# Attention and mLSTM block on one core: V, O and Z projections with time on the partitions, branch outputs turned by DMA

## Chip, cores and metric

The kernel runs on one core of a Trainium2 chip. The metric is the device time of one execution in microseconds; the median of several runs is given, and a profiled execution supplies the trace.

## What is computed

One layer of a hybrid block on x (1024 time steps, 1024 channels), batch 1, everything in float32 at the interface:

```
xn = rmsnorm(x)
(da_q, da_k, da_v, da_z, ml_q, ml_k, ml_v, ml_o, ml_z, ml_i, ml_f, gate_a, gate_m) = split(xn @ w_in)
y_a = diff_attention(da_q, da_k, da_v) * silu(da_z)          # 8 heads, two softmaxes per head,
                                                             # rmsnorm over the head's 128 channels
y_m = mlstm(conv_silu(ml_q), conv_silu(ml_k), ml_v, ml_i, ml_f)   # 8 heads, chunked, layer norm per head
y_m = sigmoid(ml_o) * y_m * silu(ml_z)
merged = sigmoid(gate_a) * (y_a @ w_pa) + sigmoid(gate_m) * (y_m @ w_pm)
out = rmsnorm(x + merged @ w_out)
```

Each head has 128 value channels, and 1024 steps are eight blocks of 128. Every large product is done in float16 with both operands split into a high and a low half: high x high, high x low and low x high are accumulated, three matmuls where one would do in one precision.

## The kernel before

**Layout.** X, the normed input, lies in SBUF turned: channels on the partitions, time along the row, as f16 high and low halves. A *unit* (class `Unit`) is 256 output columns of a projection: two blocks of 128. `plain_unit` (lines 334 to 346) computes it with the weights stationary and X moving: for each half of the time (`th`, 512 steps) and each block (`cb`), 8 channel blocks x 3 matmuls of 512 columns are accumulated in one of three PSUM banks (`pp`), so a unit is 96 matmuls, and its result has output channels on the partitions and time along the row. `post` of the unit's consumer then empties the bank on ScalarE and VectorE.

**Units and consumers.** `c_avz` takes attention's V and Z of one head. V is split into f16 halves (lines 559 and 560) in `vT` and turned to rows (time on the partitions) by one transposing DMA (line 634). Z is gated in place by tanh (lines 545 and 546). `c_mvo` takes the mLSTM's V and O: V is copied to `vT` (line 345) and turned by eight TensorE transposes (`to_rows`, line 554) and a scaled ScalarE copy (line 555); O multiplies into the z gate (lines 696 and 697). `c_mz` does Z of two mLSTM heads. `c_aqk` and `c_mqk` do the Q and K projections.

**Side work.** Beside the projection of the next head runs a generator of the current one: `attention(h, plan)` or `mlstm(h)`. Lists such as `PLAN_A` give the slot (about three matmuls of projection) at which each piece is traced. In attention the piece `v` multiplies probabilities by V (lines 867 to 869) into a single PSUM bank (`pvp`) holding four blocks of time; `f` computes factors on GpSimd (lines 874 to 876); `o` scales the bank into `on` (line 880), with time on the partitions; `t` turns it by four TensorE transposes (line 885), and `finish_y` multiplies by the gate (line 528) and splits into the f16 halves of `Y` (lines 529 and 530). In the mLSTM the normed rows `num` (line 987) are turned by four TensorE transposes (line 992) into the same `finish_y`.

**Order.** Y is first read by the units `pa` and `pm`, which multiply by `w_pa` and `w_pm`; the former follow the last attention head, the latter the last mLSTM head. The final projection `wo` has the merged result stationary (128x128) and 256 columns of weights moving. Weights of a unit are loaded into three buffers (line 226, by SyncE's queue), squared and summed for a scale (ScalarE, line 245), and split (lines 257 and 259) while the unit before is computed. Work is traced in program order and then placed on each engine's in-order queue by the framework's planner, which goes by modelled times, so that the order on an engine can differ from the program's. SyncE's queue holds nearly all DMA issues: weight loads, the Q and K copies, attention's transposing DMAs (line 859).

Of the kernel before, what the change touches and what calls it, by code (L numbers as in the profile page):

```python
# [9 lines left out]
F16 = mybir.dt.float16  # L10
# [7 lines left out]
P = 128  # L18
# [30 lines left out]
def block_kernel(ctx, tc, x, norm_w, w_in, lam, subln_w, rel_bias, conv_w, conv_b, b_if,  # L49
# [38 lines left out]
    def p_ps():  # L88
        return pp.tile([P, 512], F32, tag="pp", name=nm("pp"))
# [4 lines left out]
    def m_ps():  # L94
        return pmi.tile([P, 512], F32, tag="pmi", name=nm("pmi"))
# [7 lines left out]
    def b3(ap):  # L103
        return ap.rearrange("p (a b) -> p a b", b=P)
# [168 lines left out]
    def wplain(w, i, c):  # L273
        hi, lo = w.parts[i // 2]
        return hi[:, i % 2, c], lo[:, i % 2, c]
# [16 lines left out]
        return t[:, 0, i % 2, :], t[:, 1, i % 2, :]  # L292

    def y_src(base):
        return lambda i, th: (Y[base + i][:, 0, th, :], Y[base + i][:, 1, th, :])

    class Unit:
        def __init__(self, kind, idx, srcs, rowscale=None, src=x_src, keep=False):
            self.kind, self.idx, self.srcs = kind, idx, srcs
            self.rowscale, self.src, self.keep = rowscale, src, keep  # L300
            self.w = self.prepping = None

        def start_load(self):
# [30 lines left out]
    def plain_unit(w, dst, post, src):  # L334
        for th in range(2):
            for cb in range(2):
                c = slice(cb * P, (cb + 1) * P)
                ps = p_ps()
                yield from mm3(ps, KC, lambda i: wplain(w, i, c),
                               lambda i: src(i, th), True, True)  # L340
                d = dst(cb, th) if dst else None
                if d is None:
                    d = ps
                else:
                    s.activation(d, ps, AF.Copy)  # L345
                post(cb, th, d)

    HS = [slice(0, 512), slice(512, 1024)]

    def wcols(o, n=P):  # L350
        return (w_in[0, :, o:o + n], n)
# [168 lines left out]

    isz = ctile([P, 16], p="isz")

    def finish_y(n, ps, th, gz, k):

        if n not in Y:
            Y[n] = xtile("Y")
        y32 = half_tile("y32")
        v.scalar_tensor_tensor(y32, ps, 2.0 ** k, gz[:, HS[th]], op0=ALU.mult, op1=ALU.mult)
        s.activation(Y[n][:, 0, th, :], y32, AF.Copy)
        v.tensor_tensor(Y[n][:, 1, th, :], y32, Y[n][:, 0, th, :], op=ALU.subtract)  # L530

    def sig_of(w):
        sg = sm(p="sig", bufs=8)
# [5 lines left out]
        v.tensor_scalar(hs, sg, 0.5, None, op0=ALU.mult)  # L539
        return hs  # L540

    def gate_post(tz, th, ap, hs):

        t = HS[th]
# [3 lines left out]
    def to_rows(src, dst, sg):  # L548

        def part(th):  # L550
            tp = m_ps()
            for j in range(4):
                c = th * 4 + j
                te.transpose(tp[:, j * P:(j + 1) * P], src[:, c * P:(c + 1) * P], ident)
            s.activation(dst[:, th * 4:th * 4 + 4, :P], b3(tp), AF.Copy, scale=sg)
        return [lambda: None, lambda: None, lambda: part(0), lambda: part(1)]
# [5 lines left out]
    def to_rows16(src, dst):  # L562

        def part(th):
            tp = m_ps()
            for j in range(4):
                c = th * 4 + j
                te.transpose(tp[:, j * P:(j + 1) * P], src[:, c * P:(c + 1) * P], ident)
            split16(dst, b3(tp), slice(th * 4, th * 4 + 4))
        return [lambda: None, lambda: None, lambda: part(0), lambda: part(1)]  # L570


    live = {}
# [41 lines left out]
    def c_avz(h, w):  # L615
        sg = sig_of(w)
        hs = half_of(sg)
        v.tensor_scalar(isz[:, h:h + 1], sg, 0.8 * 0.5 * 2.0 ** 17, None, op0=ALU.mult)
        tz = R(p="tz")
        vT, vr = R(F16, [P, 2, S], p="vT"), R(F16, [P, 2, NT, P], p="vr")  # L620
# [6 lines left out]
        done = [0]  # L627

        def post(cb, th, ap):
            if cb == 0:  # L630
                split16(vT, ap, HS[th])
                done[0] += 1
                if done[0] == 2:
                    nc.sync.dma_start(vr.rearrange("p a b c -> p (a b) c"), vT.rearrange("p a b -> p (a b)"),
                                      transpose=True)
            else:
                gate_post(tz, th, ap, hs)
        return None, post

    def c_mqk(h, w):  # L640
# [34 lines left out]
    def c_mvo(h, w):  # L675
        sg = sig_of(w)
        hs = half_of(sg)
        vT = R(p="vT")
# [8 lines left out]
        done = [0]  # L687

        def post(cb, th, ap):
# [8 lines left out]
        return (lambda cb, th: vT[:, HS[th]] if cb == 0 else None), post  # L698

    def c_mz(h, w):  # L700
        sg = sig_of(w)
        hs = half_of(sg)
        tz = [R(p="tz") for _ in range(2)]
# [3 lines left out]
        return None, lambda cb, th, ap: gate_post(tz[cb], th, ap, hs)  # L707
# [101 lines left out]
    def attention(h, plan):  # L809
# [67 lines left out]

        def scaled_of(qh):
            on[qh] = half_tile("on")
            v.tensor_tensor(b3(on[qh]), b3(ops[qh]), fac[qh].unsqueeze(2).to_broadcast([P, 4, P]), op=ALU.mult)  # L880

        def rows_of(qh):
            tp = m_ps()
            for j in range(4):
# [15 lines left out]
    def mlstm(h):  # L900
# [83 lines left out]
        for th in range(2):  # L984
            for c in range(th * 4, th * 4 + 4):
                with tc.high_priority(50):
                    v.tensor_scalar(num[:, c, :P], num[:, c, :P], va[:, c:c + 1], nmr[:, c:c + 1], op0=ALU.mult,
                                    op1=ALU.add)
            yield
            tp = m_ps()  # L990
            for j in range(4):
# [22 lines left out]
    def scale_m():  # L1014
# [3 lines left out]

    da_units = lambda h: [
        Unit("aqk", h, [wcols(OFF_DA[0] + h * P), wcols(OFF_DA[1] + h * P)]),  # L1020
        Unit("avz", h, [wcols(OFF_DA[2] + h * P), wcols(OFF_DA[3] + h * P)])]
    ml_units = lambda h: (
        [Unit("mqk", h, [wcols(OFF_ML[0] + h * P), wcols(OFF_ML[1] + h * P)])]
        + ([Unit("mz", h, [wcols(OFF_ML[4] + h * P, 256)])] if h % 2 == 0 else [])
        + [Unit("mvo", h, [wcols(OFF_ML[2] + h * P), wcols(OFF_ML[3] + h * P)])])
# [54 lines left out]
    for units, side, steps in phases:  # L1080
# [6 lines left out]
        for u in units:  # L1087
# [7 lines left out]
            gen = plain_unit(u.w, dst, post, u.src)  # L1095
            if n == 0:
                ifp = if_proj()
                gen = itertools.chain(gen, ifp)
# [136 lines left out]
```

## Time and profile before

| | |
|---|---|
| median of 3 runs | 1446.03 us (1445.68 to 1446.54) |
| profiled execution, its own time | 1444.22 us |
| its span, first to last instruction | 1442.4 us |
| granted TensorE clock, mean | 0.998 of full speed |
| TensorE busy | 1391.0 us, 7922 matmuls |
| VectorE, ScalarE, GpSimd busy | 844.3, 728.7, 156.5 us |
| DMA, transfers of the main queue | 32.7% of 16 engines' span |

The engines are PE (TensorE matmuls), PEld (its weight loads, which overlap), DVE (VectorE), ACT (ScalarE), POOL (GpSimd) and SP (SyncE, here only the issuing of DMAs). A row names the source line, engine, operation, output and inputs by the program's names. A busy time is the sum of a group's records; records of matmuls overlap, so the distance between starts is what one costs in a stream.

### The profile page before, as it was taken

Reading aid. Unit: us, or ns where it says so; the run is one execution under the profiler, and the core shown is the slowest. Engines: PE = TensorE matmul, PEld = TensorE weight load, DVE = VectorE, ACT = ScalarE, POOL = GpSimd, SP = SyncE. Lnnn points to the kernel's source line nnn. Section 1 sums busy time; section 2 is a strip of 40 time slices with the busy share of each in tenths; the row PEclk is TensorE's granted clock in tenths of the full one; section 3 lists DMA queues with packets and bytes.
Section 4 is the critical chain, followed back from the end, with each engine's and each line's share of the span. In section 5 each row is a group of like instructions: output and inputs, shape, how many; then the busy total and the mean of one; then the engine's idle time right before and its main releaser. Section 6 shows DMA issues by size and latency. Waiting matters only on the chain.

```text
span 1442.4 us, 21396 instructions
## 1 busy us (share of the span) xinstructions
PE 1391.0 (96%) x7922; PEld 748.4 (52%) x7922; DVE 844.3 (59%) x2214; ACT 728.7 (51%) x1469; POOL 156.5 (11%) x215
## 2 busy tenths in 40 slices
PE   5999999999999999999999999999999999999997
PEld 3445455455554545444455556455555555444686
DVE  6286967759677577333537565665665654233633
ACT  6275666556665577522444354343434344634542
POOL 2001001010010001000111111010111200122004
PEclk9999999999999999999999999999999999999999
DMA  6575557355464544434312121121212124434303
GB/s 198 71 165 127 102 109 148 83 120 112 103 141 87 112 105 141 163 128 129 95 30 88 30 88 59 54 64 44 74 30 88 59 70 145 165 95 167 119 15 118
DMA packets 215419, 145.72 MB, mean 101 GB/s; under 512 B 100145, under 2 KB 192578, under 8 KB 215314
## 3 DMA queue, kind: packets, MB, share of 16 engines
q1 hardware_dynamic: 201298, 119.08, 32.7%
q10 hardware_dynamic: 14016, 25.27, 5.2%
q8 instruction: 62, 1.02, 0.3%
q14 instruction: 43, 0.35, 0.1%
HBM read 90.12 MB, written 18.55 MB: 75 GB/s over the span
## 4 chain that ended last, share of the span: by engine, by line
PE 70%; DVE 14%; ACT 5%; DMA 4%; POOL 3%; issue 3%; SPq 0%; POOLq 0%; DVEq 0%; ACTq 0%
PE pp L329 20%; PE pp L331 20%; PE pp L330 20%; PE psb L824 3%; DVE z L834 2%; DVE wp L259 2%; DVE acc L657 2%; DMA wt<-in_w_in_dram 1%; DMA qw<-rows_d 1%; DMA z<-z 1%; PE psb L920 1%; ACT z L838 1%; ACT junk L245 1%; DVE z L849 1%; PE pvp L867 1%
## 5 line engine op out<-in xcount | busy, mean ns | idle before, releaser
L331 PE MATMUL pp<-X,wp 128*128 128x512 f16 x1408 | 533.6, 379 | 1.0 <-DVE wp L259 1.0
L329 PE MATMUL pp<-X,wp 128*128 128x512 f16 x1408 | 534.0, 379 | 0.3 <-ACT wp L257 0.3
L330 PE MATMUL pp<-X,wp 128*128 128x512 f16 x1408 | 534.0, 379 | 0.0
L331 PEld LDWEIGHTS <-wp 128*128 128x128 f16 x1664 | 162.7, 98 | 190.4 <-DVE wp L259 1.5
L329 PEld LDWEIGHTS <-wp 128*128 128x128 f16 x1664 | 162.8, 98 | 172.0 <-issue 5.3
L330 PEld LDWEIGHTS <-wp 128*128 128x128 f16 x1664 | 162.7, 98 | 162.6
L257 ACT ACTIVATE wp<-wt,sb 128x512 f16<-128x512 f32 x208 | 137.0, 711 | 112.8 <-DVE sb L138 79.6
L245 ACT ACTIVATE junk<-wt 128x1024 bf16<-128x1024 f32 x112 | 118.2, 1055 | 122.9 <-DMA wt<-in_w_in_dram 113.0
L259 DVE SCALAR_TENSOR_TENSOR wp<-wt,sb,wp 128x512 f16<-128x512 f32 x208 | 149.2, 752 | 14.7 <-ACT wp L257 13.2
L838 ACT ACTIVATE z<-z,mx 128x256 f32<-128x256 f32 (+7 forms) x128 | 98.6, 770 | 49.1 <-DVE mx L837 37.4
L834 DVE CUSTOM_DVE_ANT_0 z<-psb,BB,negc 128x256 f32<-128x256 f32 (+7 forms) x128 | 104.2, 814 | 11.2 <-PE psb L824 9.5
L331 PE MATMUL pp<-Y,wp 128*128 128x512 f16 x256 | 97.0, 379 | 0.0
L330 PE MATMUL pp<-Y,wp 128*128 128x512 f16 x256 | 97.0, 379 | 0.0
L329 PE MATMUL pp<-Y,wp 128*128 128x512 f16 x256 | 97.0, 379 | 0.0
L657 DVE SCALAR_TENSOR_TENSOR acc<-up,wcol,acc 128x512 f32<-128x512 f32 x96 | 77.0, 817 | 26.3 <-POOL acc L658 23.8
L824 PE MATMUL psb<-K,Q 128*128 128x512 f16 (+3 forms) x384 | 83.2, 325 | 5.5 <-DVE mx L834 2.9
L159 DVE TENSOR_TENSOR s<-wss 128x1 bf16<-128x1 f32 x57 | 14.2, 249 | 117.3 <-ACT junk L245 117.1
L658 POOL TENSOR_SCALAR acc<-up,wcol,cols 128x512 f32<-128x512 f32 x32 | 30.8, 966 | 394.3 <-ACT up L345 231.3
L329 PE MATMUL pp<-wo,M 128*128 128x256 f16 x256 | 69.8, 273 | 0.5 <-DVE xr L1177 0.5
L331 PE MATMUL pp<-wo,M 128*128 128x256 f16 x256 | 69.8, 273 | 0.0
L330 PE MATMUL pp<-wo,M 128*128 128x256 f16 x256 | 69.8, 273 | 0.0
L824 PEld LDWEIGHTS <-Q 128*128 128x128 f16 x384 | 37.1, 97 | 54.7 <-issue 18.1
(244 smaller groups left out, 1764.9 us busy)
## 6 DMA issues: line engine op xcount, KB each, us to landing
wt<-in_w_in_dram SPq DMA_DIRECT2D x128, 256.0 KB, 3.5
wt<-in_w_in_dram SPq DMA_DIRECT2D x24, 512.0 KB, 4.3
K<-hl SPq DMA_DIRECT2D x32, 256.0 KB, 4.1
gate_d<-tg ACTq DMA_DIRECT2D x32, 256.0 KB, 2.0
xt<-in_x_dram SPq DMA_DIRECT2D x8, 512.0 KB, 6.2
Q<-hl SPq DMA_DIRECT2D x32, 128.0 KB, 2.8
wt<-in_w_pa_dram SPq DMA_DIRECT2D x8, 512.0 KB, 5.3
ft<-gate_d ACTq DMA_DIRECT2D x16, 256.0 KB, 3.1
```

Of the source, the lines that this page charges most:

```text
L245: s.activation(j, w.wt[k], AF.Square, accum_out=ss[:, k:k + 1])
L257: s.activation(dst[0], src, AF.Copy, scale=w.sb)
L259: v.scalar_tensor_tensor(dst[1], src, w.sb, dst[0], op0=ALU.mult, op1=ALU.subtract)
L329: te.matmul(ps, wh, xh, start=(start and i == 0), stop=False, **kw)
L330: te.matmul(ps, wh, xl, start=False, stop=False, **kw)
L331: te.matmul(ps, wl, xh, start=False, stop=(stop and i == n - 1), **kw)
L657: tap = lambda j: (lambda: v.scalar_tensor_tensor(a, sh(j), wc(j), a, op0=ALU.mult, op1=ALU.add))
L658: yield lambda: g.tensor_scalar(a, sh(0), wc(0), bc, op0=ALU.mult, op1=ALU.add)
L824: te.matmul(sp[:, c:e], Q[:, p, i * P:(i + 1) * P], K[p][:, j, c:e], start=(j == 0), stop=(j == 1))
L834: v.tensor_tensor_reduce(z[:, :n], sp[:, :n], bb[:, S - n:], negc, BIG, op0=ALU.add, op1=ALU.min, accum_out=mx)
L838: s.activation(z[:, :n], z[:, :n], AF.Exp, bias=mx, scale=-1.0, accum_out=rr[:, 2 * i + p:2 * i + p + 1])
L849: v.scalar_tensor_tensor(A[:, :n], E[i, 1][:, :n], nb, A[:, :n], op0=ALU.mult, op1=ALU.add)
```

## The change

The projections whose consumers want time on the partitions are computed that way. A new `rows_unit` has X stationary (128 time steps) and 256 weight columns moving; a PSUM bank holds two time blocks x 256 columns, and `post` gets a pair of time blocks at a time. It is used for avz, mvo and mz. So V comes out as rows and the vT tiles, their transposing DMA and `to_rows` go, and the gates z and o are rows too. The branch outputs are gated while still rows (inside `scaled_of` in attention, by one multiplication in the mLSTM), split into f16 halves in a tile `y16`, and turned into Y by one transposing DMA for each half of the time. Y's layout is [half of time, high or low] in place of [high or low, half of time].

```diff
+    def rows_unit(w, post, src):
+        both = slice(0, 2 * P)
+        for n in range(NT // 2):
+            ps = p_ps()
+            for j in range(2):
+                o = slice(j * 2 * P, (j + 1) * 2 * P)
+                t = slice((n % 2 * 2 + j) * P, (n % 2 * 2 + j + 1) * P)
+                for i in range(KC):
+                    (wh, wl), (xh, xl) = wplain(w, i, both), src(i, n // 2)
+                    te.matmul(ps[:, o], xh[:, t], wh, start=i == 0, stop=False)
+                    te.matmul(ps[:, o], xh[:, t], wl, start=False, stop=False)
+                    te.matmul(ps[:, o], xl[:, t], wh, start=False, stop=i == KC - 1)
+                    if i % 2 == 1:
+                        yield
+            ps = ps.rearrange("p (j c) -> p j c", j=2)
+            for cb in range(2):
+                post(cb, slice(2 * n, 2 * n + 2), ps[:, :, cb * P:(cb + 1) * P])
...
-    def finish_y(n, ps, th, gz, k):
+    def finish_y(n, th, y32, k):
...
-        y32 = half_tile("y32")
-        v.scalar_tensor_tensor(y32, ps, 2.0 ** k, gz[:, HS[th]], op0=ALU.mult, op1=ALU.mult)
-        s.activation(Y[n][:, 0, th, :], y32, AF.Copy)
-        v.tensor_tensor(Y[n][:, 1, th, :], y32, Y[n][:, 0, th, :], op=ALU.subtract)
+        y16 = half_tile("y16").bitcast(F16)
+        s.activation(y16[:, :512], y32, AF.Copy, scale=2.0 ** k)
+        v.scalar_tensor_tensor(y16[:, 512:], y32, 2.0 ** k, y16[:, :512], op0=ALU.mult, op1=ALU.subtract)
+        nc.sync.dma_start(Y[n][:, th].rearrange("p a (c t) -> p (a c) t", t=P), y16, transpose=True)
...
     c_avz:
-                split16(vT, ap, HS[th])
-                done[0] += 1
-                if done[0] == 2:
-                    nc.sync.dma_start(vr.rearrange("p a b c -> p (a b) c"), vT.rearrange("p a b -> p (a b)"),
-                                      transpose=True)
+                split16(vr, ap, t)
             else:
-                gate_post(tz, th, ap, hs)
+                gate_post(tz, t, ap, hs)
...
     c_mvo:
-                done[0] += 1
-                if done[0] == 2:
-                    bg.extend(to_rows(vT, vr, sg))
+                s.activation(vr[:, t, :P], ap, AF.Copy, scale=sg)
             else:
-                to = main_tile("to")
+                to = main_tile("to")[:, :2 * P].rearrange("p (a b) -> p a b", b=P)
                 s.activation(to, ap, AF.Tanh, scale=hs)
-                v.scalar_tensor_tensor(gz[:, HS[th]], to, 1.0, gz[:, HS[th]], op0=ALU.add, op1=ALU.mult)
+                v.scalar_tensor_tensor(gz[:, t], to, 1.0, gz[:, t], op0=ALU.add, op1=ALU.mult)
...
     attention:
         def scaled_of(qh):
             on[qh] = half_tile("on")
-            v.tensor_tensor(b3(on[qh]), b3(ops[qh]), fac[qh].unsqueeze(2).to_broadcast([P, 4, P]), op=ALU.mult)
+            for j in range(4):
+                i = qh * 4 + j
+                v.scalar_tensor_tensor(on[qh][:, j * P:(j + 1) * P], ops[qh][:, j * P:(j + 1) * P],
+                                       fac[qh][:, j:j + 1], gz[:, i], op0=ALU.mult, op1=ALU.mult)
         def rows_of(qh):
-            tp = m_ps()
-            for j in range(4):
-                te.transpose(tp[:, j * P:(j + 1) * P], on[qh][:, j * P:(j + 1) * P], ident)
-            finish_y(h, tp, qh, gz, -17)
+            finish_y(h, qh, on[qh], -17)
...
     mlstm:
-            tp = m_ps()
-            for j in range(4):
-                te.transpose(tp[:, j * P:(j + 1) * P], num[:, th * 4 + j, :P], ident)
-            finish_y(8 + h, tp, th, gz, -18)
+            y32 = half_tile("y32")
+            v.tensor_tensor(b3(y32), num[:, th * 4:th * 4 + 4, :P], gz[:, th * 4:th * 4 + 4], op=ALU.mult)
+            finish_y(8 + h, th, y32, -18)
```

## Rows read from the trace of the kernel before

**Rows 1.** The page's first part: busy us, share of span, instruction counts by engine.
```profile
PE 1391.0 (96%) x7922; PEld 748.4 (52%) x7922; DVE 844.3 (59%) x2214; ACT 728.7 (51%) x1469; POOL 156.5 (11%) x215
```

**Rows 2.** Windows, attention then mLSTM stretch: length, engines' busy us, granted clock, DMA share, GB/s.
```profile
60.00:557.00 497.00, 479.02 (x2932) 247.57 (x2931) 357.53 (x949) 308.21 (x677) 37.42 (x62) 1.00 0.54 119
700.00:1225.00 525.00, 517.39 (x2733) 281.52 (x2732) 311.10 (x862) 223.09 (x412) 61.99 (x77) 1.00 0.22 67
```

**Rows 3.** TensorE's waits, whole span: line, releaser, total us, times, longest us.
```profile
PE pmi L554 <- ACT vT L345: 7.2, 4, 2.1
PE pvp L867 <- DVE nbeta L846: 7.2, 6, 1.4
...
PE pvp L867 <- DVE on L880: 3.1, 2, 1.6
```

**Rows 4.** Timeline of TensorE in an mvo unit: start us, length us, instruction.
```profile
740.61 0.38 PE L330 MATMUL pp<-X,wp 128*128 128x512 f16 x1
...
742.12 0.38 PE L331 MATMUL pp<-X,wp 128*128 128x512 f16 x1
742.33 0.60 PE L554 MATMUL pmi<-ident,vT 128*128 128x128 f32 x4
742.77 0.38 PE L329 MATMUL pp<-X,wp 128*128 128x512 f16 x1
```

**Rows 5.** Timeline of TensorE in the final projection, eleven matmuls left out between.
```profile
1353.18 0.27 PE L329 MATMUL pp<-wo,M 128*128 128x256 f16 x1
...
1354.49 0.27 PE L329 MATMUL pp<-wo,M 128*128 128x256 f16 x1
```

**Rows 6.** Instructions by line and shape: busy us, mean ns, idle before; a load, a transpose.
```profile
L330 PEld LDWEIGHTS <-wp 128*128 128x128 f16 x1664 | 162.7, 98 | 162.6
...
L554 PE MATMUL pmi<-ident,vT 128*128 128x128 f32 x64 | 9.8, 276 | 7.2 <-ACT vT L345 7.2
```

**Rows 7.** Timeline around the fifth block row of one attention head, wait in brackets.
```profile
174.97 0.84 POOL L874 TENSOR_SCALAR fac<-ssq,eps 128x4 f32<-128x4 f32 x1 [43.38 <-ACT junk L870]
...
177.21 0.69 DVE L880 TENSOR_TENSOR on<-pvp,fac 128x512 f32<-128x512 f32 x1 [0.86 <-POOL fac L876]
...
178.05 0.22 PE L867 MATMUL pvp<-vr,z 128*128 128x128 f16 x1 [1.16 <-DVE nbeta L846]
```

**Rows 8.** Instructions by line and shape on VectorE, all reading PSUM.
```profile
L942 DVE SCALAR_TENSOR_TENSOR C<-C,decb,pmi 128x129 f32<-128x129 f32 x48 | 16.6, 346 | 15.0 <-PE pmi L939 15.0
...
L1177 DVE SCALAR_TENSOR_TENSOR xr<-pp,so,xr 128x256 f32<-128x256 f32 x32 | 15.4, 481 | 30.8 <-PE pp L331 30.8
...
L560 DVE SCALAR_TENSOR_TENSOR vT<-pp,vT 128x512 f16<-128x512 f32 x16 | 11.0, 688 | 17.7 <-ACT vT L559 17.7
...
L880 DVE TENSOR_TENSOR on<-pvp,fac 128x512 f32<-128x512 f32 x16 | 11.0, 685 | 8.8 <-POOL fac L876 8.8
```

**Rows 9.** Timeline of VectorE and ScalarE in the mvo unit of mLSTM head 1.
```profile
788.96 0.74 DVE L259 SCALAR_TENSOR_TENSOR wp<-wt,sb,wp 128x512 f16<-128x512 f32 x1
...
790.74 1.06 ACT L245 ACTIVATE junk<-wt 128x1024 bf16<-128x1024 f32 x1 [3.61 <-DMA wt<-in_w_in_dram]
...
793.61 1.06 ACT L245 ACTIVATE junk<-wt 128x1024 bf16<-128x1024 f32 x1 [1.72 <-DMA wt<-in_w_in_dram]
...
799.53 0.69 ACT L696 ACTIVATE to<-pp,hs 128x512 f32<-128x512 f32 x1 [2.34 <-PE pp L331]
```

**Rows 10.** Timeline: the last split of attention's last Y, and Y's first reader.
```profile
580.97 1.30 DVE L530 TENSOR_TENSOR Y<-y,Y 128x512 f16<-128x512 f32 x2 [2.41 <-ACT Y L529]
...
598.67 0.38 PE L329 MATMUL pp<-Y,wp 128*128 128x512 f16 x1
```

**Rows 11.** DMA issues: attention's transposing DMAs, their count, us from issue to landing.
```profile
z<-z SPq DMA_TRANSPOSE x64, 3.5
```

**Rows 12.** Waits of SyncE's queue, whole span: line, releaser, total us, times, longest.
```profile
SPq L226 <- DVE wp L259: 541.6, 76, 23.8
...
SPq L634 <- DVE vT L560: 51.2, 7, 7.9
```

More of the change, by code (lines that the diff above doesn't have):

```diff
@@ L294, in y_src, with __init__ @@
     def y_src(base):
-        return lambda i, th: (Y[base + i][:, 0, th, :], Y[base + i][:, 1, th, :])
+        return lambda i, th: (Y[base + i][:, th, 0, :], Y[base + i][:, th, 1, :])
     class Unit:
-        def __init__(self, kind, idx, srcs, rowscale=None, src=x_src, keep=False):
+        def __init__(self, kind, idx, srcs, rowscale=None, src=x_src, keep=False, rows=False):
             self.kind, self.idx, self.srcs = kind, idx, srcs
-            self.rowscale, self.src, self.keep = rowscale, src, keep
+            self.rowscale, self.src, self.keep, self.rows = rowscale, src, keep, rows
             self.w = self.prepping = None
@@ L540, in half_of, with gate_post @@
         return hs
-    def gate_post(tz, th, ap, hs):
-        t = HS[th]
+    def gate_post(tz, t, ap, hs):
         s.activation(tz[:, t], ap, AF.Tanh, scale=hs)
         v.scalar_tensor_tensor(tz[:, t], tz[:, t], 1.0, ap, op0=ALU.add, op1=ALU.mult)
-    def to_rows(src, dst, sg):
-        def part(th):
-            tp = m_ps()
-            for j in range(4):
[L553 to L556, printed above, removed]
     def split16(dst, src, sl):
@@ L560, in split16 @@
         v.scalar_tensor_tensor(dst[:, 1, sl], src, 2.0 ** -13, dst[:, 0, sl], op0=ALU.mult, op1=ALU.subtract)
-    def to_rows16(src, dst):
-        def part(th):
-            tp = m_ps()
-            for j in range(4):
[L567 to L570, printed above, removed]
     live = {}
@@ L618, in c_avz @@
         v.tensor_scalar(isz[:, h:h + 1], sg, 0.8 * 0.5 * 2.0 ** 17, None, op0=ALU.mult)
-        tz = R(p="tz")
-        vT, vr = R(F16, [P, 2, S], p="vT"), R(F16, [P, 2, NT, P], p="vr")
+        tz = R(shape=[P, NT, P], p="tz")
+        vr = R(F16, [P, 2, NT, P], p="vr")
         eps = sm(p="eps")
@@ L626, in c_avz, with post @@
         live["vz", h] = (vr, tz, eps)
-        done = [0]
-        def post(cb, th, ap):
+        def post(cb, t, ap):
             if cb == 0:
-                split16(vT, ap, HS[th])
-                done[0] += 1
-                if done[0] == 2:
-                    nc.sync.dma_start(vr.rearrange("p a b c -> p (a b) c"), vT.rearrange("p a b -> p (a b)"),
-                                      transpose=True)
+                split16(vr, ap, t)
             else:
-                gate_post(tz, th, ap, hs)
+                gate_post(tz, t, ap, hs)
         return None, post
@@ L677, in c_mvo @@
         hs = half_of(sg)
-        vT = R(p="vT")
         vr = R(shape=[P, NT, P + 1], p="vr")
@@ L686, in c_mvo, with post @@
         gz = live["z", h]
-        done = [0]
-        def post(cb, th, ap):
+        def post(cb, t, ap):
             if cb == 0:
-                done[0] += 1
-                if done[0] == 2:
-                    bg.extend(to_rows(vT, vr, sg))
+                s.activation(vr[:, t, :P], ap, AF.Copy, scale=sg)
             else:
-                to = main_tile("to")
+                to = main_tile("to")[:, :2 * P].rearrange("p (a b) -> p a b", b=P)
                 s.activation(to, ap, AF.Tanh, scale=hs)
-                v.scalar_tensor_tensor(gz[:, HS[th]], to, 1.0, gz[:, HS[th]], op0=ALU.add, op1=ALU.mult)
-        return (lambda cb, th: vT[:, HS[th]] if cb == 0 else None), post
+                v.scalar_tensor_tensor(gz[:, t], to, 1.0, gz[:, t], op0=ALU.add, op1=ALU.mult)
+        return None, post
     def c_mz(h, w):
@@ L702, in c_mz @@
         hs = half_of(sg)
-        tz = [R(p="tz") for _ in range(2)]
+        tz = [R(shape=[P, NT, P], p="tz") for _ in range(2)]
         for k in range(2):
@@ L706, in c_mz @@
         live["z", h], live["z", h + 1] = tz
-        return None, lambda cb, th, ap: gate_post(tz[cb], th, ap, hs)
+        return None, lambda cb, t, ap: gate_post(tz[cb], t, ap, hs)
     gate_d = dram.tile([2, KC, P, S], F32, tag="gated", name="gate_d")
@@ L989, in mlstm @@
             yield
-            tp = m_ps()
-            for j in range(4):
-                te.transpose(tp[:, j * P:(j + 1) * P], num[:, th * 4 + j, :P], ident)
-            finish_y(8 + h, tp, th, gz, -18)
+            y32 = half_tile("y32")
+            v.tensor_tensor(b3(y32), num[:, th * 4:th * 4 + 4, :P], gz[:, th * 4:th * 4 + 4], op=ALU.mult)
+            finish_y(8 + h, th, y32, -18)
             yield
@@ L1020, in block_kernel @@
         Unit("aqk", h, [wcols(OFF_DA[0] + h * P), wcols(OFF_DA[1] + h * P)]),
-        Unit("avz", h, [wcols(OFF_DA[2] + h * P), wcols(OFF_DA[3] + h * P)])]
+        Unit("avz", h, [wcols(OFF_DA[2] + h * P), wcols(OFF_DA[3] + h * P)], rows=True)]
     ml_units = lambda h: (
         [Unit("mqk", h, [wcols(OFF_ML[0] + h * P), wcols(OFF_ML[1] + h * P)])]
-        + ([Unit("mz", h, [wcols(OFF_ML[4] + h * P, 256)])] if h % 2 == 0 else [])
-        + [Unit("mvo", h, [wcols(OFF_ML[2] + h * P), wcols(OFF_ML[3] + h * P)])])
+        + ([Unit("mz", h, [wcols(OFF_ML[4] + h * P, 256)], rows=True)] if h % 2 == 0 else [])
+        + [Unit("mvo", h, [wcols(OFF_ML[2] + h * P), wcols(OFF_ML[3] + h * P)], rows=True)])
     ga = [Unit("ga", j, [wcols(OFF_GATE[0] + j * P, 256)]) for j in range(0, KC, 2)]
@@ L1094, in block_kernel @@
             dst, post = consumers[u.kind](u.idx, u.w)
-            gen = plain_unit(u.w, dst, post, u.src)
+            gen = rows_unit(u.w, post, u.src) if u.rows else plain_unit(u.w, dst, post, u.src)
             if n == 0:
```

2 lines of the change are left out of this document (removed).

## The prediction

> **What bounds the kernel now.** First the page's busy shares: TensorE is busy 96% of the span, the next engine, VectorE, 59% [rows 1]. A busy TensorE is no proof by itself, since its records overlap, so the second view is the busy time by stretch: in the attention stretch TensorE has 479 of 497 us, in the mLSTM stretch 517 of 525, with the granted clock at 1.00, the level of 2.4 GHz; VectorE has 358 and 311 [rows 2]. The third view is TensorE's own waits [rows 3]: the largest in the middle of the kernel are 7.2 us in front of the transposes of line 554 and 7.2 + 3.1 us in front of the probability-times-V matmuls of line 867. So TensorE's queue sets the time nearly everywhere, and a microsecond taken off it comes off the end, unless it becomes a wait. ScalarE, VectorE, SyncE and the DMA engines matter only where TensorE waits for them.
>
> **Part 1, the 192 transposes (lines 554, 885, 992, 64 each).** The 276 ns of one record [rows 6] is mostly latency. The cost is the spacing: a group of four starts at 742.33 and the next projection matmul at 742.77 [rows 4], 0.44 us. 48 groups x 0.44 = **21.1 us off TensorE**.
>
> **Part 2, the 20 units turned to rows** (8 avz, 8 mvo, 4 mz). Each goes from 96 matmuls of 512 columns to 192 of 256, each with its weight load. At 512 columns, 740.61 to 742.12 is seven steps, 0.2157 us each [rows 4]. At 256 columns the last projection has the very form, a stationary 128x128 f16 block and 256 moving f16 columns: 1353.18 to 1354.49 is twelve steps, 0.1092 us each [rows 5]. A unit goes from 96 x 0.2157 = 20.71 to 192 x 0.1092 = 20.97 us; 20 units: **+5.2 us**. A unit now reads all its split weights in its first 2.6 us, not 5.2. In a row unit's neighbourhood the last split of the next unit's weights ended at 789.70 and the unit before it at about 799.5, where ScalarE was waiting for its last bank [rows 9]: ten microseconds of slack, so no cost.
>
> **Part 3, the wait for vT.** Line 554 waited 7.2 us in four places for the ScalarE copy of vT [rows 3]; copy and transposes both go. What is late next there is ScalarE itself: it stands 3.6 and 1.7 us in front of the squares of a weight tile whose DMA has not landed [rows 9], and the emptying of projection banks queues behind that. There are three banks, each filled in 48 x 0.109 = 5.2 us, so a bank may stay full for 10.5 us, and ScalarE is held some 7.6 (787.1 to 794.7). I take **-7.2 us**; bounds 0 (the wait reappears) and -7.2.
>
> **Part 4, gating before turning, attention.** The bank of line 867 is single: the fifth block row's matmuls wait until `scaled_of` has read the first four. At 178.05 TensorE has stood 1.16 us for the product begun at 177.21 and done at 177.90, behind the GpSimd factors begun at 174.97 [rows 7]; the row names another VectorE instruction, but the end of line 880 is what frees the bank. The product becomes four instructions of 128 columns. The nearest row is the 128x129 product from PSUM at 346 ns: 4 x 0.346 = 1.38 against 0.69 us [rows 8], +0.69 in each of 8 heads. Between 0 (the planner puts more projection matmuls ahead) and +5.5 us I take the middle, **+2.8**, since nothing in the trace says which. VectorE's sum stays: a head had two products and two multiplications by z of 512 columns (4 x 0.69) and has 8 x 0.346.
>
> **Part 5, smaller evacuations.** Every bank is emptied by four operations of 256 elements, not two of 512; on VectorE 481 ns at 256 against 688 [rows 8]. Per head two such pairs change: 2 x (4 x 0.481 - 2 x 0.688) = +1.1 us, 17.5 over 16 heads, on an engine with 844 us of 1442; ScalarE likewise. It lies beside TensorE, and the three banks are the cover; where that fails, attention's chain of softmax steps is hit. Cost 0 to +3, taken as **+1**.
>
> **Part 6, DMA and SyncE.** 32 transposing DMAs of 128x1024 f16 come, 8 of 128x2048 go. Attention's own land 3.5 us after issue [rows 11]. No reader is near: head 7's Y halves were done at 582.3 and the first matmul on Y starts at 598.67 [rows 10], its own block being read 21 matmuls later. On SyncE, weight loads stand in front of them, which wait up to 23.8 us for a buffer [rows 12]; behind them, weight loads, Q/K copies and attention's transposes wait while a Y transpose waits for VectorE. The removed vT transposes waited 51.2 us in 7 places, at most 7.9 [rows 12], and TensorE's waits show nothing of it. Cost 0; without that cover it is rival (b).
>
> The Trainium skill's page "VectorE: DVE Perf Modes" (section "The three transpose paths") speaks against this part: it gives a 128x128 bf16 transpose 390 ns on TensorE and 1309 ns by DMA, and would use TensorE where PSUM will do. The rows agree that the DMA is the slower path and differ on the other price; as an estimate, the page's 390 ns would make the removal worth 75 us, not 21.1, and the median 1373.
>
> **Sum.** -21.1 + 5.2 - 7.2 + 2.8 + 1.0 = -19.3 us. The profiled execution has a span of 1442.4 us in a time of 1444.22; the median of the runs is 1446.03, 1.8 above it. Span 1423.1, median 1446.03 - 19.3 = **1427**. Bounds: -23.1 with the costs at nothing (1423), -7.4 with every cost at its end and no wait saved (1439). A new order of instructions could also take up to some 6 of the 10.3 us at line 867 (1417).
>
> **Rivals.**
> (a) *Smaller gain.* The vT wait moves to the emptying of banks, line 867 pays fully, VectorE costs 3: -7.4, 1439. If head 7's Y also sits behind a weight load that waits 24 us (issued at 606, landed at 609.5, wanted at 603.2), 6 more: 1445, no change. For it: attention's account is thin (8 heads x (8 x 0.11 - 0.26) = 5 us against up to 5.5). Against: the mLSTM half holds most of the gain.
> (b) *Slower: SyncE holds the weights.* Place: mLSTM phases, 16 Y transposes, each waiting up to 7.9 us as vT's did, ahead of a weight load. ScalarE, held 7.6 us in front of the squares already, is held 15.5, five more than the banks cover. All 16: 80 us, 1507; it decides from four of the 16 on. Against: vT's did the same in attention and cost TensorE nothing.
> (c) *It doesn't do what it says: with half the columns behind each, the weight loads show.* A load is recorded at 98 ns [rows 6], beside a step of 109: little room. Bounds from rows: nothing shows (0.1092 us a step), or every load does, 3840 x 0.098 = 376 us, 1803. The sign turns at 5 ns per matmul (19.3 / 3840). Against: rows 5 has the same shape with nothing showing.
> The Trainium skill's page "TensorE: Matmul & The Clock Gate" ("Back-to-back issue gap") has a rule on (c)'s side: in a stream of load and matmul pairs both set the spacing, ~131 ns at 512 columns and ~81 at 128. The rows have 215.7 at 512 and 109.2 at 256 and follow that section's other formula, N/2.4 + 2.5, in which loads stay hidden.
>
> **How the numbers follow.** Forecast, 1419 to 1434: 0.73. (a) 0.17, of which 0.13 still faster and 0.04 no change. (b) 0.04, (c) 0.02. A larger gain, below 1419: 0.04. A measurement here tells 0.2%, 2.9 us, from no change. Faster 0.73 + 0.13 + 0.04 = 0.90, same 0.04, slower 0.06. The range 1417 to 1438 takes in the forecast, half of the larger gain and most of (a).
>
> **What would show it.** Lines 554, 885 and 992 gone, and the waits of 554; row-unit matmuls 109 ns apart; TensorE busy some 16 us less; at line 867 a wait of 1.2 to 1.9 us per head; some 18 us gained in the mLSTM stretch, attention within 3 us of before; no TensorE wait on Y. Wrong would be: a spacing over 114 ns, row matmuls waiting on ScalarE or VectorE for a bank, or a wait for split weights.

## The result: 1435.6 us, 10 us faster, with 10 us lost in attention

The changed kernel takes 1435.61 us (median of four runs, 1435.37 to 1436.87), the kernel before 1445.86 us on the same chip. The ratio is 0.9931, 95% interval 0.9913 to 0.9948. The profiled execution has a span of 1433.9 us, against 1442.4.

The page's first part [rows 1] and two windows [rows 2] of the changed kernel; columns as there:

```profile
PE 1380.6 (96%) x9650; PEld 913.3 (64%) x9650; DVE 848.0 (59%) x2310; ACT 735.0 (51%) x1533; POOL 157.5 (11%) x215
...
60.00:557.00 497.00, 469.25 (x3553) 309.78 (x3552) 354.70 (x1007) 309.21 (x696) 34.77 (x61) 0.99 0.53 112
700.00:1225.00 525.00, 524.11 (x3843) 386.09 (x3842) 323.08 (x916) 232.29 (x462) 65.62 (x79) 1.00 0.29 80
```

TensorE fills the mLSTM window (524 of 525 us), but in the attention window it has 10 us more idle than before (469 against 479 busy). Two landmarks of TensorE's timeline date the halves: the first matmul on Y, and the first of the final projection. In the changed kernel:

```profile
608.87 0.38 PE L329 MATMUL pp<-Y,wp 128*128 128x512 f16 x1
...
1339.14 0.27 PE L329 MATMUL pp<-wo,M 128*128 128x256 f16 x1
```

Before, they stood at 598.67 [rows 10] and 1347.38:

```profile
1347.38 0.27 PE L329 MATMUL pp<-wo,M 128*128 128x256 f16 x1
```

The stretch between went from 748.7 to 730.3 us, 18.4 shorter; all that comes before it became **10.2 us longer**.

TensorE's waits [rows 3], whole span:

```profile
PE pvp L855 <- DVE on L870: 12.0, 8, 1.6
...
PE psb L812 <- DMA K<-hl: 4.6, 2, 2.5
PE pvp L855 <- DMA z<-z: 4.2, 5, 1.1
...
PE pmi L165 <- DVE s L159: 1.6, 7, 0.2
```

Line 855 is the old 867, probabilities times V (called pV below), and 870 the old 880. The waits of 554 are gone. Row-unit matmuls run at the predicted distance [rows 5]:

```profile
256.05 0.27 PE L358 MATMUL pp<-wp,X 128*128 128x256 f16 x1
256.16 0.27 PE L359 MATMUL pp<-wp,X 128*128 128x256 f16 x1
256.27 0.27 PE L360 MATMUL pp<-wp,X 128*128 128x256 f16 x1
```

**An account of attention.** Listed waits leave out gaps that a long record covers (0.27 us long, 0.109 apart). So I took, from TensorE's timeline between the first score matmul and the first matmul on Y, each group's distance to the next, less its count times its spacing (0.2158, 0.1092 and 0.0556 us at 512, 256 and 128 columns). What is left over, by what follows:

| gaps in front of, us | before | after |
|---|---|---|
| pV | 15.0 | 22.6 |
| the second scores of the first head | 0 | 2.4 |
| all other scores | 8.6 | 11.9 |
| the weights' sum (L165) | 2.3 | 2.8 |
| row matmuls, at half the clock | 0 | 1.5 |

The difference is 15.2 us. With 64 transposes less (7.0) and eight row units more (8 x 0.26 = 2.1) that is 15.2 - 7.0 + 2.1 = 10.3, against 10.2 measured. The experiments ask what the gaps are.

### The profile page after: what moved, and what is told of

It reads as the page before. It is cut to its first block, busy times and chain, and to the rows that moved or that the text cites. A ratio compares the mean times of both kernels' runs of the same rounds, so it can differ in the third digit from the quotient of the medians.

```text
span 1433.9 us, 25050 instructions
## 1 busy us (share of the span) xinstructions
PE 1380.6 (96%) x9650; PEld 913.3 (64%) x9650; DVE 848.0 (59%) x2310; ACT 735.0 (51%) x1533; POOL 157.5 (11%) x215
## 4 chain that ended last, share of the span: by engine, by line
PE 77%; DVE 9%; ACT 4%; DMA 4%; POOL 3%; issue 3%; SPq 0%; POOLq 0%; DVEq 0%; ACTq 0%
PE pp L329 14%; PE pp L331 14%; PE pp L330 14%; PE pp L360 8%; PE pp L358 8%; PE pp L359 8%; PE psb L812 3%; DVE z L822 3%; DMA z<-z 2%; ACT z L826 1%; DMA qw<-rows_d 1%; DVE wp L259 1%; PE psb L908 1%; PE pvp L855 1%; DVE hl L600 1%
## 5 line engine op out<-in xcount | busy, mean ns | idle before, releaser
L358 PE MATMUL pp<-wp,X 128*128 128x256 f16 x1280 | 349.7, 273 | 0.0
L359 PE MATMUL pp<-wp,X 128*128 128x256 f16 x1280 | 349.7, 273 | 0.0
L360 PE MATMUL pp<-wp,X 128*128 128x256 f16 x1280 | 349.7, 273 | 0.0
L329 PE MATMUL pp<-X,wp 128*128 128x512 f16 x768 | 291.7, 380 | 0.3 <-ACT wp L257 0.3
L331 PE MATMUL pp<-X,wp 128*128 128x512 f16 x768 | 291.3, 379 | 0.6 <-DVE wp L259 0.6
L330 PE MATMUL pp<-X,wp 128*128 128x512 f16 x768 | 291.8, 380 | 0.0
L331 PEld LDWEIGHTS <-wp 128*128 128x128 f16 x1024 | 100.0, 98 | 119.7 <-DVE wp L259 1.2
L329 PEld LDWEIGHTS <-wp 128*128 128x128 f16 x1024 | 100.2, 98 | 103.0 <-issue 1.7
L330 PEld LDWEIGHTS <-wp 128*128 128x128 f16 x1024 | 100.1, 98 | 97.1
L359 PEld LDWEIGHTS <-X 128*128 128x128 f16 x1280 | 125.3, 98 | 18.4 <-issue 2.4
L358 PEld LDWEIGHTS <-X 128*128 128x128 f16 x1280 | 125.4, 98 | 16.8 <-issue 0.8
L360 PEld LDWEIGHTS <-X 128*128 128x128 f16 x1280 | 125.3, 98 | 14.6
```

Source lines behind the costliest of these rows:

```text
L329: te.matmul(ps, wh, xh, start=(start and i == 0), stop=False, **kw)
L330: te.matmul(ps, wh, xl, start=False, stop=False, **kw)
L331: te.matmul(ps, wl, xh, start=False, stop=(stop and i == n - 1), **kw)
L358: te.matmul(ps[:, o], xh[:, t], wh, start=i == 0, stop=False)
L359: te.matmul(ps[:, o], xh[:, t], wl, start=False, stop=False)
L360: te.matmul(ps[:, o], xl[:, t], wh, start=False, stop=i == KC - 1)
```

## Experiments

Each ratio is against runs of the kernel before on the same chip. The intervals reach some 2 us to either side, so two variants less than about 3 us apart are not told apart by their times alone.

### The halves alone

`ml_only` keeps attention as it was (a plain unit, V turned by DMA, the gate after TensorE's transposes), `att_only` keeps the mLSTM; the Y layout is the new one in both. The line that parts them, in `ml_only`:

```diff
-        Unit("avz", h, [...], rows=True)]
+        Unit("avz", h, [...])]
```

> Only the mLSTM half of the change (mvo and mz as row units, mLSTM outputs turned by DMA); attention as in the kernel before, Y keeps the new layout. If the two halves of the change are independent, as the traces' milestones say (first matmul on Y at 598.67 before and 608.87 after, first final-projection matmul 748.7 later before and 730.3 after): first matmul on Y back at 598.7 within 0.5, the stretch after it 730 within 1, the median 18 to 19 below before, about 1427. If the mLSTM half gained only because attention's work had moved into it, the stretch is over 735 and the median 1431 or more.

Measured: 1426.18 us, ratio 0.9863 (0.9849 to 0.9876).

> Only the attention half of the change; the mLSTM half as before. Independent halves: first matmul on Y at 608.9, the stretch after it 748.7, the median 10 above before, about 1456. If the loss in attention comes from something the whole program shares (more instructions, more DMA in all), it is smaller here, 1449 to 1453.

Measured: 1455.88 us, ratio 1.0074 (1.0061 to 1.0087). The halves are independent and add up: -19.6 and +10.1. Half of the change is worth more than all of it. In `ml_only` the first landmark stands at 598.21, where it was before (598.67), and the second at 1328.54, 730.3 later:

```profile
598.21 0.38 PE L329 MATMUL pp<-Y,wp 128*128 128x512 f16 x1
...
1328.54 0.27 PE L329 MATMUL pp<-wo,M 128*128 128x256 f16 x1
```

### One product instead of four

```diff
-            for j in range(4):
-                v.scalar_tensor_tensor(on[...], ops[...], fac[qh][:, j:j + 1], gz[:, i], ...)
+            v.tensor_tensor(b3(on[qh]), b3(ops[qh]), fac[qh].unsqueeze(2)..., op=ALU.mult)
 ...
+            v.tensor_tensor(b3(on[qh]), b3(on[qh]), gz[:, qh * 4:qh * 4 + 4], op=ALU.mult)
```

> The changed kernel, but attention's gate is taken out of the four products that free the bank of the probability-times-V matmuls: one product of 512 columns by the factors as before, and one multiplication by z from SBUF when the half is turned. Theory 'bank' (the bank is held 0.7 us longer per head, and that is the loss): the wait in front of the fifth block row falls from 1.6 to 1.2 us or less per head, the wait for the transposed block 7 stays at 1.0 or falls, and the median falls by 3 to 6 us, to 1430 to 1433. Theory 'order' (the queue was laid out by modelled times in which a row matmul is longer than it is): the queue puts fewer row matmuls in front of the fifth block row too (30 in place of 37), so the wait stays 1.4 to 1.7 and the median within 2 us of 1435.6.

Measured: 1436.55 us, ratio 0.9932 (0.9919 to 0.9946), as the changed kernel. Its waits:

```profile
PE pvp L855 <- DVE on L868: 11.9, 7, 1.8
```

The product is 0.6 us shorter and the wait is no shorter, since the planner now lays 30 row matmuls between the fourth and the fifth block row instead of 37 (7 x 0.109 = 0.76 us). The four products are not what attention lost by.

### Y turned by TensorE

```diff
         def rows_of(qh):
-            finish_y(h, qh, on[qh], -17)
+            ...
+            tp = m_ps()
+            for j in range(4):
+                te.transpose(tp[...], on[qh][...], ident)
+            ...
```

> The changed kernel, but attention's gated rows are turned by four TensorE transposes for each half, as before, so attention's 16 Y transposing DMAs and their place on SyncE's queue are gone; the row units and the gate in the products stay. If DMA and SyncE cost nothing (the prediction's part 6) the time is the changed kernel's plus 64 transposes at 0.11 us = 7.0 us: 1440 to 1445. If the Y transposes on SyncE are what makes attention 10 us longer, it is 1426 to 1434.

Measured: 1440.05 us, ratio 0.9955 (0.9940 to 0.9969), 4.4 us above the changed kernel. By the account above the 64 transposes cost their 7.0 us, and the gaps in attention's stretch are 2.3 us smaller (39.4 against 41.7 in all). Attention's transposing DMAs and their place on SyncE cost at most the 2.6 us that are missing to 7.0, and they are not the 10 us.

### A later last block row: half of the loss

```diff
-PLAN_A = [..., (31, 'v6'), (31, 'v7'), (42, 't0'), ...]
+PLAN_A = [..., (31, 'v6'), (42, 'v7'), (42, 't0'), ...]
```

> The changed kernel with one entry of PLAN_A moved: v7 (probabilities times V of the last block row) from slot 31 to 42. TensorE's queue then has 49 matmuls of 256 columns between v6 and v7 instead of 24; the kernel before had 16 of 512 columns there, 3.45 us against 2.62 now. Theory 'thin cover': the 4.2 us at L855 <- DMA z and the small gaps in front of v7 are new because the same transposed probabilities are wanted 0.8 us sooner; they go, and nothing takes their place, since the wait of v4 (12.0 us) lies ahead of it: 1429.5 to 1432.5. Rival 'the head is one chain': what v7 no longer waits shows up as a longer wait elsewhere in the head, 1434 to 1437.

Measured: 1430.27 us, ratio 0.9888 (0.9873 to 0.9903): **5.3 us** back, as "thin cover" said; the gaps in front of pV fell by 5.6. The wait for the transposed probabilities is gone, that of the fifth block row stands untouched:

```profile
PE pvp L855 <- DVE on L870: 12.1, 8, 1.6
```

The two timelines show why it was there. Before: the last projection matmul ahead of the last block row, its first matmul, and on SyncE the DMA that turns its probabilities.

```profile
186.17 0.38 PE L330 MATMUL pp<-X,wp 128*128 128x512 f16 x1
186.40 0.23 PE L867 MATMUL pvp<-vr,z 128*128 128x128 f16 x1
...
181.87 2.05 SPq L859 DMA_TRANSPOSE z<-z  x1
```

The same after:

```profile
192.60 0.27 PE L359 MATMUL pp<-wp,X 128*128 128x256 f16 x1
193.86 0.23 PE L855 MATMUL pvp<-vr,z 128*128 128x128 f16 x1 [0.98 <-DMA z<-z]
...
188.90 2.97 SPq L847 DMA_TRANSPOSE z<-z  x1
```

The DMA is issued 3.8 us after the fifth block row's first matmul in both (178.05 to 181.87, 185.12 to 188.90): it is not later. In this head its record is longer too (2.97 against 2.05 us), but over the seven heads that use this list the mean is 2.24 us after and 2.39 before. What changed is the work laid between: between the seventh block row and the last stood 16 projection matmuls of 512 columns, 16 x 0.2157 = 3.45 us, and now 24 of 256, 24 x 0.109 = 2.62. **The cover became 0.8 us thinner while the matmuls became more.** The counts, 16 against 24, look as if the planner priced a 256-column matmul at two thirds of a 512-column one, 0.144 us; the chip takes 0.109. That price is inferred from the counts; what the planner computes was not looked at. Giving it a later slot removed the loss.

### A later fifth block row: the wait moves

```diff
-PLAN_A = [..., (28, 'v3'), (29, 'v4'), (29, 'v5'), (30, 'f0'), (30, 'o0'), (31, 'v6'), (31, 'v7'), ...]
+PLAN_A = [..., (28, 'v3'), (30, 'f0'), (30, 'o0'), (36, 'v4'), (36, 'v5'), (37, 'v6'), (42, 'v7'), ...]
```

> The changed kernel with four numbers of attention's slot list altered: block rows 4 to 7 of the probability-times-V matmuls are traced at slots 36, 36, 37, 42 in place of 29, 29, 31, 31, so TensorE's queue holds 54 row matmuls in front of block row 4 (37 in the changed kernel) and 25 in front of block row 7 (24, and 17 more in front of all of them). Theory 'order': the waits of 1.6 us (bank) and 1.0 us (transposed block 7) vanish in the seven heads that use this list, 7 x 2.5 = 17 us, median 1417 to 1422. Theory 'bank' alone: only the 1.6 goes, 7 x 1.6 = 11, about 1424. Theory 'DMA' (transposing Y on the same queue delays block 7 itself): the second wait stays, since block 7 lands later too; about 1424 to 1427.

Measured: 1428.10 us, ratio 0.9875 (0.9862 to 0.9888): less of a gain than any of the three theories said, and only 2 us below `later_v7`, which the intervals do not tell apart. By the account above the gaps in front of pV fell from 22.6 to 5.7 us, and those in front of line 165 rose from 2.8 to 12.2:

```profile
PE pmi L165 <- DVE s L159: 11.1, 7, 1.7
...
PE pvp L855 <- DVE on L870: 1.5, 1, 1.5
```

Line 165 needs `s`, which stands on VectorE behind the very products that wait for the factors, and a combine of 1.27 us. In `later_v`:

```profile
182.57 0.61 DVE L870 SCALAR_TENSOR_TENSOR on<-pvp,fac,tz 128x128 f32<-128x128 f32 x2 [1.54 <-POOL fac L864]
...
185.00 0.15 DVE L159 TENSOR_TENSOR s<-wss 128x1 bf16<-128x1 f32 x1
```

The chain of one head in the changed kernel [rows 7]: the square of the fourth block row on ScalarE, the factors, the first and last product, and the fifth block row's first matmul.

```profile
180.96 0.35 ACT L858 ACTIVATE junk<-pvp,rc 128x128 bf16<-128x128 f32 x1
...
181.51 0.83 POOL L862 TENSOR_SCALAR fac<-ssq,eps 128x4 f32<-128x4 f32 x1 [44.92 <-ACT junk L858]
...
183.75 0.61 DVE L870 SCALAR_TENSOR_TENSOR on<-pvp,fac,tz 128x128 f32<-128x128 f32 x2 [1.53 <-POOL fac L864]
...
184.72 0.35 DVE L870 SCALAR_TENSOR_TENSOR on<-pvp,fac,tz 128x128 f32<-128x128 f32 x1
...
185.12 0.22 PE L855 MATMUL pvp<-vr,z 128*128 128x128 f16 x1 [1.59 <-DVE on L870]
```

The fourth block row's last matmul started at 179.27, so its square began 1.69 us later, behind an exponential and a split copy on ScalarE. Before, that was 0.55 us (173.87 and here):

```profile
174.42 0.35 ACT L870 ACTIVATE junk<-pvp,rc 128x128 bf16<-128x128 f32 x1
```

From that matmul to the fifth block row it is 5.85 us instead of 4.18, and cover rose from 13 x 0.2157 = 2.80 to 37 x 0.109 = 4.04.

### Attempts on that chain

`early_v3` multiplies the fourth block row ahead of the last row's softmax:

```diff
-PLAN_A = [..., (24, 'r6'), (25, 'q7'), (27, 'r7'), (28, 'v3'), (29, 'v4'), ...]
+PLAN_A = [..., (22, 'v3'), (24, 'r6'), (25, 'q7'), (27, 'r7'), (29, 'v4'), ...]
```

> The changed kernel with one entry of PLAN_A moved: v3 (probabilities times V of the fourth block row) from slot 28 to 22, ahead of row 7's softmax. Theory 'ScalarE queue': in the changed kernel the square of that block row (L858) begins 1.69 us after its last matmul (179.27 to 180.96) because row 7's exponential and a split copy stand in front of it on ScalarE; before it was 0.55 us. The factors, the products and the fifth block row's matmuls follow it, so the wait of 12.0 us at L855 <- on is late work on ScalarE. With v3 ahead of these the wait falls to under 3 us and the time to 1423 to 1428. Rival 'price': the planner lays only as many 256-column matmuls under the wait as it thinks needed, and overprices them, so the wait forms again wherever the piece is put: wait at L855 still 9 us or more, time 1433 to 1438. The wait for the transposed probabilities of the last block row (4.2 us) is left alone by both.

Measured: 1438.04 us, ratio 0.9941 (0.9925 to 0.9957). The wait on `on` fell as said, to 1.5 us, and the time did not. Two other waits have grown in its place, in front of pV (4.2 before this edit) and in front of the scores (2.3):

```profile
PE pvp L855 <- DMA z<-z: 11.2, 12, 1.3
PE psb L812 <- DVE mx L822: 9.9, 17, 1.6
```

My expectation had counted the wait and not what its place covers. `early_v3_late_v4` moves the later pieces as well:

```diff
+PLAN_A = [..., (22, 'v3'), ..., (26, 'f0'), (26, 'o0'), ..., (34, 'v4'), (34, 'v5'), (35, 'v6'), (40, 'v7'), ...]
```

> The changed kernel with PLAN_A moved at both ends: v3 to slot 22, f0 and o0 to 26, v4 and v5 to 34, v6 to 35, v7 to 40. With v4 to v7 alone moved later (later_v, 1428.1 us) the wait at line 855 went, but a wait of 1.6 us per head came up at L165 <- s (11.1 us in 7 places): the weights' scale queues on VectorE behind the products, which wait for the factors. Theory 'ScalarE queue': that is the same late square one step on, so with v3 early both waits are gone: waits at L855 and L165 together under 5 us, time 1416 to 1422. Rival: the wait at L165 has another source (weights that land late, or VectorE's own load) and stays near 11 us: 1426 to 1430.

Measured: 1431.18 us, ratio 0.9895 (0.9880 to 0.9911). The waits on `on` (one of 1.5 us is left) and at 165 are gone as one theory said, but the scores wait 9.7 us for VectorE and pV 3.8 for squares, so the time is that of neither.

`later_v_pool` is `later_v` with `s` on GpSimd:

```diff
-            v.tensor_tensor(s16, ss[:, 0:1], ss[:, 1:2], op=ALU.add)
+            g.tensor_tensor(s16, ss[:, 0:1], ss[:, 1:2], op=ALU.add)
```

> later_v (1428.1 us) and one thing more: the sum of a weight tile's two squares (L159, s) is done on GpSimd instead of VectorE. In later_v TensorE waits 1.66 us per head at L165 for s (11.1 us in 7 places), and VectorE has s behind four products of line 870 and a 1.27 us combine, 1.4 us after the squares are done. Theory 'VectorE's queue, held by the late factors': s no longer stands behind them, the wait at L165 falls to under 6 us, time 1419 to 1423. Rival: the wait is the squares on ScalarE themselves, or goes to v4 instead: 1426 to 1430.

Measured: 1426.95 us, ratio 0.9868 (0.9852 to 0.9883). The wait at 165 fell to 4.5 us, so `s` did wait behind the products, and pV got a wait that the rival had foreseen; the time is the rival's:

```profile
PE pvp L855 <- ACT junk L858: 7.8, 7, 1.3
...
PE pmi L165 <- POOL s L159: 4.5, 7, 1.1
```

The sixth block row now waits some 1.1 us per head (7.8 in seven) for the fifth's square, which reads other columns of the same bank and stands on ScalarE behind the weights' split, made earlier by the earlier `s`. The Trainium skill's page "PSUM — Partial Sum Buffer" ("PSUM bank collisions raise a hardware error") has two engines kept apart in a bank whatever columns they touch; that this wait is there for that reason is inferred from the tiles.

`later_prep` is `later_v` with the preparation of weights four slots later, which also puts the scores back in their old order:

```diff
         yield
         yield
+        yield
+        yield
+        yield
+        yield
         w.sb = sm(p="sb")
```

> The changed kernel with v4 to v7 later, as in later_v (1428.1 us), and the preparation of a unit's weights begun four slots later (four empty steps ahead of the sum s and its matmul, L159 and L165), for all units. In TensorE's queue the weights' matmul of line 165 then stands behind v4, and the score matmuls (qk) of a head stand as in the kernel before, the last of them ahead of v3 instead of in its middle. Theory 'order, not row units': what is left of attention's loss in later_v comes from these two places: 12.2 us of gaps in front of line 165, and 4 us more of small gaps and 2.4 us more at the first head in front of the score matmuls than before. Most of both goes with nothing in its place: 1410 to 1417, the fastest of all. Rival 'row units': half the columns behind each load, and four products for one, cost attention this wherever the pieces stand: 1424 to 1430. A preparation that is four slots later for the mLSTM's units too may cost TensorE a wait for split weights there; that would show at lines 358 to 360 and 329 to 331.

Measured: 1445.0 us, ratio 0.9999 (0.9989 to 1.0010): both theories missed. Attention's stretch, from the first score matmul to the first matmul on Y, took 524.2 us against 525.7 in `later_v`. In `later_prep` the gaps in front of line 165 went (12.2 to nothing), those in front of pV came back (5.7 to 16.1), most of them a wait for squares, and those in front of the scores stayed (14.5 and 15.0). Line 859 is the 855 of the other listings:

```profile
PE pvp L859 <- ACT junk L862: 11.3, 7, 1.6
```

The stretch from there to the final projection took 15 us more, through waits in the mLSTM:

```profile
PE psb L949 <- ACT num L955: 8.0, 5, 2.9
...
PE psb L951 <- DVE C L934: 3.9, 7, 0.7
```

So the old order of the scores does not bring attention's time back. A knob for all units could not tell more than that.

### A version that beats both

Old attention, new mLSTM, and cover for the waits that the kernel before has itself at line 867: v4 to v7 at 36, 37, 38 and 46, `s` on GpSimd. `ml_only_early_v3` tries the early fourth block row instead:

```diff
+PLAN_A = [..., (24, 'v3'), ..., (28, 'f0'), (28, 'o0'), (32, 'v4'), (33, 'v5'), (34, 'v6'), (38, 'v7'), ...]
```

> Only the mLSTM half of the change (1426.2 us as ml_only), with attention as in the kernel before but PLAN_A moved: v3 to slot 24, f0 and o0 to 28, v4 32, v5 33, v6 34, v7 38. Theory 'ScalarE queue': the kernel before already pays 10.3 us at line 867 for the same chain, from the fourth block row's square to the fifth's matmuls, so the wait goes here too: waits there under 3 us, time 1415 to 1419, the fastest of all if attention's row units bring nothing. Rival 'price': with 512-column matmuls the planner prices right and the wait is its choice; it moves to another place and the time stays at 1424 to 1428.

Measured: 1430.32 us, ratio 0.9887 (0.9870 to 0.9904), 4 us above `ml_only` and above both theories, with `PE psb L827 <- DVE mx` at 12.7 us (9.9 in `early_v3`).

`ml_only_later_pool` is the version named first:

```diff
+PLAN_A = [..., (30, 'f0'), (30, 'o0'), (36, 'v4'), (37, 'v5'), (38, 'v6'), (42, 't0'), (46, 'v7'), ...]
```

> Only the mLSTM half (ml_only, 1426.2 us), with attention as in the kernel before, v4 to v7 at slots 36, 37, 38 and 46, and s (L159) on GpSimd. In TensorE's queue 27 matmuls of 512 columns then stand between v3 and v4 instead of 13 (5.8 us instead of 2.8) and row 7's softmax stays ahead of v3. Theory 'thin cover': most of ml_only's 14.8 us of gaps in front of the probability-times-V matmuls goes without a new wait, 1413 to 1418. Rival: as with the early v3 of attention (1430.3), the waits come up at other lines of the head: 1423 to 1428.

Measured: **1420.93 us**, ratio 0.9831 (0.9816 to 0.9845). Gaps in front of pV fell from 14.8 to 4.5 us, but those in front of line 165 rose from 2.3 to 9.5: between the two theories, and the fastest kernel here.

```profile
PE pmi L165 <- POOL s L159: 8.4, 7, 1.4
```

## Why the prediction held, and where its steps failed

The forecast was 1427 and the time 1435.6, on the right side and inside the range of 1417 to 1438, 9 us above the forecast and just outside its own band, 1419 to 1434. Rival (a) said 1439. The size was nearer to (a), the mechanisms were not (a)'s: the wait for vT did not move, line 867's wait grew by 1.7 us and not by 5.5, and head 7's Y waited on nothing. That the time lies in the range is partly luck: the range goes up to 1438 to take in (a), and most of attention's loss, which no part of the prediction names, filled that place.

- **Parts 1 and 3, the mLSTM half**, held. The stretch lost 18.4 us where "some 18" was said. It is 128 x 0.11 = 14.1 for transposes, 12 x 0.26 = 3.1 back for row units, and 7.9 us of gaps in front of line 554: 18.9. In attention 64 transposes were worth 4.4 us in all by `pe_turn`, since other gaps grew by 2.3 us as they went.
- **Part 2** held to the digit: 0.109 us, no load shows. Rival (c) is out.
- **Part 4** had the size (12.0 against 10.3 us, so +1.7; 1.6 per head where 1.2 to 1.9 was said) and the wrong reason. `one_product` shows that the four products do not set it. The trace points to a late square and to the planner's cover: `early_v3` and `later_v` each took the wait down to 1.5 us, and other waits rose in its place.
- **Part 5** was priced from 481 ns per 256 elements; the new operations take 419 to 424 on VectorE. All operations of this kind take 53.8 us there (lines 564, 568 and 685) where they took 43.9 (546, 560 and 697): 9.9 more and not 17.5. VectorE's whole busy sum rose by 3.7. By shape, the product of line 870 among them:

```profile
L564 DVE SCALAR_TENSOR_TENSOR tz<-tz,pp 128x256 f32<-128x256 f32 x64 | 26.8, 419 | 19.7 <-ACT tz L563 19.6
...
L870 DVE SCALAR_TENSOR_TENSOR on<-pvp,fac,tz 128x128 f32<-128x128 f32 x64 | 19.4, 344 | 24.8 <-POOL fac L864 24.3 <-POOL up L639 0.5
...
L685 DVE SCALAR_TENSOR_TENSOR tz<-to,tz 128x256 f32<-128x256 f32 x32 | 13.6, 424 | 40.9 <-ACT to L684 40.9
...
L568 DVE SCALAR_TENSOR_TENSOR vr<-pp,vr 128x256 f16<-128x256 f32 x32 | 13.4, 421 | 38.4 <-ACT vr L567 38.4
```

- **Part 6** held: Y transposes wait on SyncE, the longest kind 52.7 us in five places, and no TensorE wait on Y follows. Rival (b) is out.

```profile
SPq L549 <- DVE tz L564: 52.7, 5, 15.3
```

- **The step that failed** is "attention within 3 us of before". Its sum (-7.0 + 2.1 + 2.8 + 1 = -1.1) held the work and one wait, and took the planner's layout as given. Missing were the last block row's thinner cover (5.3 us, shown by `later_v7`), the first head's second score wait and the half clock there (2.4 + 1.5 us, below; no run took them away), and 3.3 us more of small gaps in front of the other scores, whose cause stays open. The sentence "A new order of instructions could also take up to some 6 of the 10.3 us at line 867 (1417)" saw that the order could change and counted it only as a gain.
- "TensorE busy some 16 us less" came out at 10.4, though the work fell by that much. Records overlap, so gaps shorter than a record count as busy; this is argued, not shown.

The Trainium skill's page "VectorE: DVE Perf Modes" ("The three transpose paths") gives 390 ns for a bf16 transpose on TensorE; as an estimate from it, 64 would be worth 64 x 0.39 = 25 us, and `pe_turn` has 4.4. The Trainium skill's page "TensorE: Matmul & The Clock Gate" ("Back-to-back issue gap") has a spacing of ~81 ns at 128 columns; pV's matmuls are 55.6 ns apart, as by that section's other formula, N/2.4 + 2.5 (55.8).

## What to carry to other kernels

When a change replaces matmuls that lie under other waits, count cover in microseconds for each wait, not only the engine's total: as many columns in smaller pieces can leave a thinner stretch in the same place. Where one engine's in-order queue ties a chain together, a wait that is removed at one line is likely to come up at the next; add up all gaps of the stretch before and after, and try the two halves of a change apart.

## Not expected of the hardware

**The clock fell in a wait that had left it alone before.** In the changed kernel TensorE stands for 0.50 us ahead of line 165's matmul at 74.23, is idle from 74.4 to 76.86 us, runs two score matmuls, and waits 2.10 us more for K. Before, 27 projection matmuls lay between these two pairs of score matmuls; now there is none. The clock fell in the first of the two long waits: the window from 74 to 76 has 0.95, the next, in which the scores start, 0.50. Windows of 2 us; the next to last columns are the granted clock and the DMA share:

```profile
74.00:76.00 2.00, 0.16 (x1) 0.00 (x0) 1.65 (x13) 1.96 (x5) 0.25 (x1) 0.95 0.97 197
76.00:78.00 2.00, 0.37 (x2) 0.21 (x2) 1.85 (x6) 1.97 (x3) 0.00 (x0) 0.50 1.00 246
...
80.00:82.00 2.00, 2.00 (x11) 1.40 (x10) 2.00 (x8) 1.72 (x7) 0.00 (x0) 0.50 1.08 299
82.00:84.00 2.00, 2.00 (x18) 1.64 (x16) 0.88 (x4) 1.06 (x3) 0.00 (x0) 0.85 1.12 304
```

At 0.50, the 1.2 GHz level, row matmuls start 0.214 us apart:

```profile
80.14 0.42 PE L358 MATMUL pp<-wp,X 128*128 128x256 f16 x1
80.36 0.42 PE L359 MATMUL pp<-wp,X 128*128 128x256 f16 x1
```

Fourteen of them cost 14 x 0.105 = 1.5 us. Before, and in `ml_only`, TensorE also stood for some 2.6 us there and the clock stayed at 1.00. In the profiled executions of all ten kernels here with attention's row units it falls near this place (in `later_prep` at 83 us), also where the 0.50 us ahead of line 165 are missing, as in `pe_turn`; in the four with plain units it stays. What makes the difference was not tried.

**Small gaps.** In front of a pV matmul with no wait listed, TensorE is 0.12 us late after a 512-column matmul (179.66, 181.43 before) and 0.22 after a 256-column one (186.72, 188.50 after). What makes the difference was not tried.
